# Hybrid gMLP and SSD layer: squares of the last groups three ticks later, a new order of PSUM banks, the fifth unit's normalization behind two evictions, and a new turn of places for the late loads

## The chip, the cores and the metric

The kernel runs on one core of a Trainium2 chip. The metric is the device time of one execution in microseconds. A core has TensorE (PE; its weight loads are shown as PEld), VectorE (DVE), ScalarE (ACT), GpSimd (POOL), and SyncE (SP), whose queue issues most DMAs here. Each engine works through its own instructions in order; across engines they wait for each other by semaphores.

## The reference

One layer, one sequence of 1024 rows, width 1024, all in float32.

```python
h = rms_norm(x, norm_w) * (1 + scale) + shift          # scale, shift, gate from silu(c) @ ada_w + ada_b
gm_u, gm_v, gm_z, ssm_z, xbc, dt_raw, g_a, g_b = split(h @ w_in)
y_a = spatial_gating(gelu(gm_u), gelu(gm_v)) * silu(gm_z)      # chunks of 128, 8 groups
xs, bm, cm = split(silu(causal_depthwise_conv(xbc)))
y_b = ssd_scan(xs, softplus(dt_raw + dt_bias), -exp(a_log), bm, cm) + xs * d_skip
yz  = (y_b * silu(ssm_z)) as 8 groups of 256 columns
y_b = rms_norm(yz, ssm_norm_w) per group
merged = sigmoid(g_a) * (y_a @ w_proj_a) + sigmoid(g_b) * (y_b @ w_proj_b)
out = rms_norm(x + gate * (merged @ w_out), final_norm_w)
```

What matters here: each group's `yz` is squared, summed over its 256 columns, and its rows are scaled by the inverse root of that sum before the product with `w_proj_b`.

## The kernel before, in words

Products are made in float32 accuracy from high and low halves: three matmuls stand for one (`hi*hi`, `hi*lo`, `lo*hi`). Larger products use seven block products (`p1` to `p7`) in place of eight. The stages in time:

- to about 920 us: conditioning, the input projections (L591, L703), convolution and gates;
- about 920 to 1149 us: the SSD scan, 32 steps of a group and a double chunk (8 groups, two by two, 4 steps each), with the products of `w_proj_a` as a fill between them (`pma`, recorded at L91);
- 1149 to 1306 us: projection b, 56 units of 12 matmuls (L1710). A unit is one block product and one k; its four accumulators `x` or `yp` are PSUM banks;
- to the end: the output projection (`ou`, `ow`, L1968), the residual x, the last norm.

From the end of the input projections to the last unit of projection b, `hand[0]` is set: every instruction keeps the place on its engine at which the code wrote it (the wrapper at L56 records them all, so most rows of the profile have that line; matmuls go through the helper at L91, transposes through L94, SyncE's DMAs through L100). After L1906 a scheduler orders the rest.

In the SSD stage the order is set by ticks. A step `n` has three ticks: `front` (the products `yi` inside a chunk and `sp` for the state), `back` (`yn` from the state, `ym`, `y`, and `yz = y * z` on GpSimd) and `prep_products` (`pc`, `px`, from which ScalarE's copy `bn` comes). The exponentials `dcy` of the next steps go to ScalarE in the same ticks. `later(delay, f)` (L506) puts a function so many ticks ahead, and `run_tasks` (L509) runs what is due. `draw` (L1546) puts in fill.

When a group has two steps done, `post` (L1240) puts in, by ticks:

- `leave`: two stores of `yz` to DRAM (`yb_d`, SyncE);
- `squares`: ScalarE squares `yz`, GpSimd adds the two halves. For the first half row of every group (`q == 0`) the squares overwrite `yz` in its place, so they wait for the two stores;
- `post2`: matmuls `pq` with ones; `post2b`: VectorE evicts `pq` into one of three small rows, `cwt`, `tri`, `par` in turn, and SyncE stores that (`ss_d`), loads it back as `ssq`, GpSimd takes the root, SyncE stores it (`rs_d`). From there `rb` is loaded, by which `y_norm` (L1614) scales a loaded block `yn` for a unit of projection b (VectorE `yn<-yn,par,rb`, where `par` is another small tile of that name, of constants).

Banks: `bank` takes the first bank of the list `free`, `release` puts one back at its end. At the start of projection b the eight banks become `q0` to `q7`, and `places_of` (L1828) says which are the four `x` and which the four `yp` accumulators. A bank whose last content is not evicted makes its first matmul wait.

Units: `operands(u)` (L1680) makes the high half `p1bh` and the low half `p1bl` of unit u's block, the same of its weight (`p1a`), and calls `ready(u + 1)` (L1663) between, which normalizes the next unit's block. While the ticks run out, the loop at L1805 makes `operands(0)` to `operands(3)` at `n` = 2, 4, 6, 8.

Places: `gate_slot` (L1595) gives the small tiles of the gates in projection b, and the later loads of x (`xr`, L1920), a place in turn out of eight entries of three pools. A load into a place waits until its last content was read; for x that reader is GpSimd's `add_x` (L1924) or VectorE's add at L1988.

Of the kernel before, what the change touches and what calls it, by code (L numbers as in the profile page):

```python
# [21 lines left out]
NG = 8  # L22
# [13 lines left out]
def hybrid_kernel(  # L36
# [24 lines left out]
    x, out = x[0], out[0]  # L61
# [34 lines left out]
    def f32(t):  # L96
        return t.bitcast(F32)

    def move(dst, src):
        pin(nc.sync.dma_start(dst, src))  # L100
# [42 lines left out]

    hpool = tc.tile_pool(name="hpool", bufs=1, reuse_waits="tile")
    hp = hpool.__enter__()
    BANKS = (1, 2, 4, 0, 3, 6, 5, 7)
    BN = ("b11", "t1", "t2", "b22", "t3", "b21", "t4")
    bop = {}
    for nm in BN:
# [349 lines left out]
    def numbered(pool, c):  # L499
        for b in range(8):  # L500
            pool.tile([P, 512], F32, name=f"{c}{b}_0", tag=f"{c}{b}")
# [4 lines left out]
    def later(delay, f, *a):  # L506
        tasks.append((slot[0] + delay, f, a))

    def run_tasks():  # L509
        slot[0] += 1  # L510
        due = [t for t in tasks if t[0] <= slot[0]]
        for t in due:
            tasks.remove(t)
            t[1](*t[2])
# [565 lines left out]
    class Group:  # L1080
# [159 lines left out]
        def post(self, q):  # L1240

            g = self.g
            yz = self.yz[q]

            def leave():
                for j in range(2):
                    move(yb_d[2 * g + j][:, q * 512 : (q + 1) * 512], yz[:, j])

            if g < NG - 2 or q == 0:
                soon = 0 if g < NG - 2 else 4  # L1250
                later(4, leave)
                later(9 - soon, self.squares, yz, [yz[:, j] for j in range(2)])
                later(17 - 2 * soon, self.post2, q, yz[:, 0])
            else:
                wait = 1 if g < NG - 1 else 3
                later(wait + 3, leave)
                sq = [turn(r, f"sq{g}", F32) for r in ((y1_r, ym_r) if g < NG - 1 else (last_sq, last_sq))]
                later(wait, self.squares, yz, sq, pin)
                later(9, self.post2, q, sq[0])
# [79 lines left out]
    def turn(r, name, dt=F32R):  # L1339
        tags, at = r  # L1340
        at[0] += 1
        return take(name, tags[(at[0] - 1) % len(tags)], dt)
# [81 lines left out]
    p2r = None  # L1424
    for n, (name, _, _, d1, d2, g) in enumerate(todo):
# [12 lines left out]
        if n == len(jobs):  # L1438
# [6 lines left out]
            p2r = p2rpool.__enter__()  # L1445
# [9 lines left out]
        if n + 2 == len(todo):  # L1455
            wspool.__exit__(None, None, None)
            p2xpool = tc.tile_pool(name="p2x", bufs=1, side="right", reuse_waits="tile")
            p2x = p2xpool.__enter__()
# [72 lines left out]
    numbered(psum, "k")  # L1531
    free.extend(BANKS)
    for k in (6, 7):
# [12 lines left out]
    def draw(n):  # L1546
        for _ in range(n):
            left[0] -= next(fill, 1) is None
# [41 lines left out]
    def give(name):  # L1590
        room.append(tags_of.pop(name))

    n_gate = [0]

    def gate_slot(name):  # L1595
        n_gate[0] += 1
        pool, tag, b = ((p2r, "ea", 2), (p2x, "xe", 3), (p2x, "xd", 3), (p2x, "xe", 3), (p2x, "xd", 3), (p2r, "ea", 2),
                        (p2x, "xe", 3), (p2x, "xd", 3))[n_gate[0] % 8]
        return pool.tile([P, 512], F32, name=name, tag=tag, bufs=b)


# [12 lines left out]
    def y_norm(n, h):  # L1614
        t = yt[n, h]
        V.scalar_tensor_tensor(t, t, snw[:, n : n + 1], rbs[n // 2, h], op0=ALU.mult, op1=ALU.mult)

    units = [(nm, k) for nm in ("p1", "p2", "p5", "p3", "p6", "p7", "p4") for k in range(KT)]
# [4 lines left out]
    def loads(u):  # L1623

        nm, k = units[u]
        if nm in fresh:
            n, h = fresh[nm]
            y_load(n + k, h)
        aops[u] = t = big(f"{nm}a{k}", F32R).rearrange("p (v c) -> p v c", v=2)
        if nm in WB:  # L1630
            load(f32(t), wb_d[k][:, WB[nm]])
        else:
            raws[u] = raw = gate_slot(f"{nm}r{k}")
            n = k if nm == "p1" else KT + k
            load(raw, w_proj_b[n * P : (n + 1) * P, 0:512])
# [27 lines left out]
    def ready(u):  # L1663

        nm, k = units[u]
        if nm in fresh:
            n, h = fresh[nm]
            y_norm(n + k, h)
        b11, b12 = yt[k, 0], yt.get((k, 1))
        b21, b22 = yt.get((KT + k, 0)), yt.get((KT + k, 1))  # L1670
        source[u] = {"p1": b11, "p2": b21, "p5": b12, "p3": b22, "p6": b12, "p7": b11, "p4": b21}[nm]
        if nm == "p5":
            V.tensor_sub(b12, b12, b11)
        elif nm == "p6":
            V.tensor_sub(b12, b22, b12)
            give(f"yn{KT + k}_1")
        elif nm == "p7":
            V.tensor_sub(b11, b12, b11)

    def operands(u):  # L1680

        nm, k = units[u]
        t = source.pop(u)
        hi, lo = turn(bh_r, f"{nm}bh{k}"), turn(bl_r, f"{nm}bl{k}")
        A.copy(hi, t)
        if nm not in WB:
            a, raw = aops[u], raws.pop(u)
            A.copy(a[:, 0], raw)
        if u + 1 < len(units):
            ready(u + 1)  # L1690
        V.tensor_sub(lo, t, f32(hi))
        if nm not in WB:
            V.tensor_sub(a[:, 1], raw, f32(a[:, 0]))
        bops[u] = hi, lo
        if nm == "p6":
            V.tensor_sub(yt[KT + k, 0], yt[KT + k, 0], t)
        elif nm == "p7":
            give(f"yn{k}_0")
            give(f"yn{k}_1")
        elif nm == "p4":  # L1700
            give(f"yn{KT + k}_0")
# [13 lines left out]
    def gate_load(b, h):  # L1715
        hs = slice(h * 512, (h + 1) * 512)
        th = gate_slot(f"tg{b}_{h}")
        ma = kept[b, h][0] if (b, h) in kept else gate_slot(f"ma{b}_{h}")
        load(th, th_d[(KT + b) * P : (KT + b + 1) * P, hs])
        if (b, h) not in kept:  # L1720
            load(ma, mt_d[b][:, hs])
        gates[b, h] = th, ma
# [68 lines left out]
    def ahead(u):  # L1791
        if u + LOAD < len(units):
            loads(u + LOAD)
        if u + LEAD < len(units):
            operands(u + LEAD)
# [3 lines left out]
    def ya_free():  # L1799

        while emptied[0] < KT and left[0] <= 3 * (KT - 1 - emptied[0]):
            room.extend(ya_tags[emptied[0]])
            emptied[0] += 1
# [4 lines left out]
    n = 0  # L1808
    while tasks:
        n += 1  # L1810
        draw(2)
        ya_free()
        if n == 1:
            ready(0)
        elif n in (2, 4, 6, 8):
            operands(n // 2 - 1)
        if n in (4, 5, 6, 7):
            loads(n - 1)
        run_tasks()
    draw(left[0] + 1)  # L1820
    ya_free()
    for tags in (war_r[0][0][2:], wah_r[0][0][2:], wal_r[0][0][2:], y1_r[0], ym_r[0]):
        room.extend(tags)
    ps2.__exit__(None, None, None)
    ps3 = tc.tile_pool(name="ps3", bufs=1, space=PSUM, reuse_waits="tile")
    psb = ps3.__enter__()
    numbered(psb, "q")
    places_of = {"x": (0, 1, 3, 2), "y": range(4, 8)}  # L1828
    assert all(b > 3 for b in free[6:])
    OB = {"p1": 0, "p5": 1, "p7": 2, "p4": 3, "p6": 4, "p2": 5, "p3": 6}  # L1830
    OORDER = ("p1", "p5", "p6", "p7", "p4", "p3", "p2")
# [272 lines left out]
```

## Time and profile before

| | us |
|---|---|
| median of three runs | 1393.1 (1392.56 to 1395.51) |
| the profiled execution | 1396.83 |
| its span | 1395.1 |
| mean granted clock of TensorE | 0.995 |
| TensorE busy, share of the span | 98% |
| VectorE, ScalarE, GpSimd busy | 76%, 57%, 16% |
| DMA over the span | 204 GB/s |

The page's first part gives each engine's busy time. The waits of TensorE name the engine and the tile for which it stood still. A timeline row has start, duration, engine, line, operation, tiles (out<-in), form and count, and in brackets the idle time before it with what ended it; a row with a count stands for several in a run. A table of stretches has the granted clock of TensorE for each.

### The profile page before, as it was taken

What the parts mean: (1) busy time and instruction counts of PE and PEld (TensorE: products, weight loads), DVE (VectorE), ACT (ScalarE), POOL (GpSimd) and SP (SyncE); (2) the same over time, 40 slices, a digit from 0 to 9 for tenths busy, and PEclk for the clock granted to TensorE, in tenths of its full rate; (3) what the DMA queues carried; (4) which work ended last, traced back from release to release, by engine and by line L of the source; (5) the groups of instructions that cost most, each with busy time, mean ns of one, the idle gap of its engine ahead of it and who ended that gap; (6) DMA issues with size and microseconds to landing.
All of it is one profiled execution on the core that took longest, in us unless ns stands there. A gap on an engine that the chain in (4) does not pass through costs nothing.

```text
span 1395.1 us, 20387 instructions
## 1 busy us (share of the span) xinstructions
PE 1365.6 (98%) x6955; PEld 1125.6 (81%) x6955; DVE 1058.0 (76%) x1784; ACT 794.2 (57%) x1474; POOL 221.1 (16%) x209
## 2 busy tenths in 40 slices
PE   8999999999999999999999999999999899999987
PEld 7678888888888888888878887888888777888876
DVE  5666766887777678867888988578887777788965
ACT  6664456666656666655556555577877634233543
POOL 0000000000000000000000000018888870000152
PEclk9999999999999999999999999999999999999999
DMA  8565533544322356766657897598898849977452
GB/s 278 153 218 165 174 99 102 176 126 156 121 89 93 121 158 181 205 198 198 190 163 241 277 303 238 177 330 305 292 305 295 277 130 301 397 264 280 145 174 121
DMA packets 272940, 286.58 MB, mean 205 GB/s; under 512 B 18844, under 2 KB 215876, under 8 KB 272836
## 3 DMA queue, kind: packets, MB, share of 16 engines
q1 hardware_dynamic: 196676, 214.35, 48.7%
q10 hardware_dynamic: 76160, 70.92, 14.9%
q8 instruction: 55, 0.90, 0.3%
q14 instruction: 49, 0.40, 0.1%
HBM read 198.77 MB, written 86.44 MB: 204 GB/s over the span
## 4 chain that ended last, share of the span: by engine, by line
PE 82%; DVE 5%; DMA 4%; issue 3%; ACT 3%; POOL 2%; SPq 1%; ACTq 0%; DVEq 0%; POOLq 0%
PE xuz L591 6%; PE xcb L591 6%; PE x L1710 6%; PE xx L591 6%; PE xz L591 5%; PE xg L591 5%; PE yp L1710 5%; PE pma L91 4%; PE yuz L591 3%; PE ycb L591 3%; PE vx L703 3%; PE yx L591 3%; PE yz L591 3%; PE yg L591 2%; PE vy L703 2%
## 5 line engine op out<-in xcount | busy, mean ns | idle before, releaser
L56 POOL TENSOR_SCALAR_AFFINE_SELECT dcy<-dcy 128x1024 f32<-128x1024 f32 x32 | 35.4, 1107 | 782.2 <-DMA yl<-ya_d 734.6
L56 ACT ACTIVATE dcy<-dcy,nacs 128x128 f32<-128x128 f32 x256 | 78.4, 389 | 16.8 <-POOL dcy L56 16.4
L1924 POOL TENSOR_TENSOR r<-r,xr 128x512 f32<-128x512 f32 x12 | 26.6, 2236 | 160.0 <-DMA xr<-in_x_dram 152.1
L56 ACT ACTIVATE ea<-dcy 64x512 f32<-64x512 f32 x64 | 40.3, 630 | 8.1 <-DMA dcy<-acs_d 7.5
L91 PE MATMUL pma<-yh,wah 128*128 128x512 f32 x128 | 42.9, 417 | 0.0
L1029 ACT ACTIVATE ac<-ac 128x1024 f32<-128x1024 f32 x32 | 33.9, 1061 | 15.6 <-DVE ac L1027 15.5
L91 PE MATMUL pma<-yh,wal 128*128 128x512 f32 x128 | 42.6, 414 | 0.0
L56 POOL TENSOR_TENSOR yz<-y,sl 128x512 f32<-128x512 f32 x32 | 41.9, 1309 | 0.6
L56 DVE TENSOR_TENSOR dcy<-dcy,pc 128x1024 f32<-128x1024 f32 x32 | 38.9, 1216 | 2.1 <-PE pc L94 1.2
L56 DVE TENSOR_TENSOR ym<-yn,ea 128x512 f32<-128x512 f32 (+1 forms) x32 | 20.0, 624 | 26.8 <-PE yn L91 26.7
L91 PE MATMUL pma<-yl,wah 128*128 128x512 f32 x128 | 39.9, 393 | 0.0
L56 POOL TENSOR_TENSOR y<-y,ym 128x512 f32<-128x512 f32 (+1 forms) x32 | 38.4, 1199 | 9.5 <-DVE ym L56 9.4
L91 PE MATMUL yi<-dcy,xd 128*64 128x128 f32 x512 | 35.6, 282 | 0.3 <-DVE xd L56 0.3
L1027 DVE SCALAR_TENSOR_TENSOR ac<-c2cb,cwt,ac 128x1023 f32<-128x1023 f32 (+2 forms) x24 | 30.8, 1282 | 6.2 <-ACT ac L1025 6.1
L1027 DVE SCALAR_TENSOR_TENSOR ac<-c2x,cwt,ac 128x1023 f32<-128x1023 f32 (+2 forms) x24 | 30.7, 1280 | 5.2 <-ACT ac L1025 5.1
L91 PEld LDWEIGHTS yi<-dcy,xd 128*64 128x64 f32 x512 | 27.9, 139 | 6.6 <-issue 4.6
L91 PE MATMUL sp<-xe,bn 128*128 128x256 f32 x112 | 32.7, 409 | 0.0
L56 DVE SCALAR_TENSOR_TENSOR yn<-yn,par,rb 128x512 f32<-128x512 f32 x32 | 26.0, 815 | 7.8 <-DMA yn<-yb_d 7.8
L1027 DVE SCALAR_TENSOR_TENSOR ac<-c1x,cwt,ac 128x1023 f32<-128x1023 f32 (+2 forms) x24 | 30.8, 1282 | 0.7 <-ACT ac L1025 0.7
L1027 DVE SCALAR_TENSOR_TENSOR ac<-c1cb,cwt,ac 128x1023 f32<-128x1023 f32 (+2 forms) x24 | 30.8, 1282 | 0.0
L955 ACT CAST wba<-wbr 128x128 fp32r<-128x128 f32 x32 | 9.5, 296 | 36.9 <-DMA wbr<-in_w_proj_b_dram 28.8
L1844 DVE TENSOR_TENSOR wolp<-wolp,wohp 128x512 fp32r<-128x512 f32 x24 | 21.2, 904 | 11.2 <-ACT wohp L1843 11.1
(2913 smaller groups left out, 4391.8 us busy)
## 6 DMA issues: line engine op xcount, KB each, us to landing
sl<-s_d SPq DMA_DIRECT2D x32, 768.0 KB
s_d<-ac ACTq DMA_DIRECT2D x32, 512.0 KB
dcy<-acs_d SPq DMA_DIRECT2D x32, 512.0 KB
aw<-in_ada_w_dram SPq DMA_DIRECT2D x16, 512.0 KB
vp<-in_w_in_dram SPq DMA_DIRECT2D x32, 256.0 KB
wbr<-in_w_proj_b_dram SPq DMA_DIRECT2D x64, 128.0 KB
wb_d<-wbb ACTq DMA_DIRECT2D x32, 256.0 KB
wb_d<-wbc ACTq DMA_DIRECT2D x32, 256.0 KB
```

The lines of the kernel that those rows point to most:

```text
L56: return lambda *a, **k: tc.keep_in_program_order(f(*a, **k))
L91: pin(PE.matmul(acc, l, r, start=first, stop=last))
L591: pin(PE.matmul(ps, lw[:, k * P : (k + 1) * P], r[k], start=first and n + k == 0, stop=n == 2 and k == 3, skip_group_check=not first))
L703: pin(PE.matmul(ps[j], l[k][:, js], r, start=first and k + m == 0, stop=k == 3 and m == 2, skip_group_check=not first))
L955: A.copy(hl[:, :, 0], t)
L1027: V.scalar_tensor_tensor(ac[:, s:], cc[:, : S - s], conv_wt[:, 3 - s, i : i + 1], ac[:, s:], op0=ALU.mult, op1=ALU.add)
L1029: A.activation(ac, ac, AF.Silu)
L1710: pin(PE.matmul(ps[j], a[:, v, js], r, start=first and n + k == 0, stop=n == 2 and k == KT - 1, skip_group_check=not first))
L1844: V.tensor_sub(lo, f32(lo), f32(hi))
L1924: G.tensor_add(rows[t][:, half], rows[t][:, half], xr.pop((t, half.start)))
```

## The change

Four places change.

1. `post`: for the last two groups (6 and 7) and `q == 0`, the squares come 8 ticks behind, not 5, and `post2` 12, not 9.
2. `BANKS` is (1, 2, 0, 4, 3, 6, 5, 7) and the x accumulators lie in (1, 3, 0, 2), where they lay in (0, 1, 3, 2).
3. `operands(3)` no longer calls `ready(4)`; it is called once behind the loop, after the last fill.
4. `gate_slot` uses another order of places.

```diff
-    BANKS = (1, 2, 4, 0, 3, 6, 5, 7)
+    BANKS = (1, 2, 0, 4, 3, 6, 5, 7)
...
             if g < NG - 2 or q == 0:
-                soon = 0 if g < NG - 2 else 4
+                late = g >= NG - 2
                 later(4, leave)
-                later(9 - soon, self.squares, yz, [yz[:, j] for j in range(2)])
-                later(17 - 2 * soon, self.post2, q, yz[:, 0])
+                later(8 if late else 9, self.squares, yz, [yz[:, j] for j in range(2)])
+                later(12 if late else 17, self.post2, q, yz[:, 0])
...
         n_gate[0] += 1
-        pool, tag, b = ((p2r, "ea", 2), (p2x, "xe", 3), (p2x, "xd", 3), (p2x, "xe", 3), (p2x, "xd", 3), (p2r, "ea", 2),
-                        (p2x, "xe", 3), (p2x, "xd", 3))[n_gate[0] % 8]
+        pool, tag, b = ((p2x, "xd", 3), (p2x, "xe", 3), (p2r, "ea", 2), (p2x, "xd", 3), (p2x, "xe", 3), (p2x, "xd", 3),
+                        (p2x, "xe", 3), (p2r, "ea", 2))[{2: 3, 3: 2}.get(n_gate[0], n_gate[0]) % 8]
...
-    def operands(u):
+    def operands(u, then=True):
...
-        if u + 1 < len(units):
+        if then and u + 1 < len(units):
             ready(u + 1)
...
         elif n in (2, 4, 6, 8):
-            operands(n // 2 - 1)
+            operands(n // 2 - 1, n < 8)
...
     draw(left[0] + 1)
     ya_free()
+    ready(4)
...
-    places_of = {"x": (0, 1, 3, 2), "y": range(4, 8)}
+    places_of = {"x": (1, 3, 0, 2), "y": range(4, 8)}
```

On ScalarE, at the end of the SSD scan, the order of the last two groups' third and fourth steps. `yz_0_10611` are the squares of group 6, `yz_0_10701` those of group 7; `dcy` are exponentials, eight in a row, `bn` the copies that TensorE waits for.

```order
 L56 ACTIVATE ea_3_10737<-dcy_3_10733 64x512 x2
+L56 ACTIVATE dcy_3_10733<-dcy_3_10733,nacs 128x128 x8
+L56 COPY bn_2_10894<-pc_2_10867 128x256
+L56 ACTIVATE ea_3_10812<-dcy_3_10808 64x512 x2
+L56 CAST wah_0_10923<-wa_0_10363 128x512
+L56 CAST wah_1_10926<-wa_1_10365 128x512
 L56 ACTIVATE yz_0_10611<-yz_0_10611 128x512 x2
-L56 ACTIVATE dcy_3_10733<-dcy_3_10733,nacs 128x128 x8
-L56 COPY bn_2_10897<-pc_2_10867 128x256
-L56 ACTIVATE ea_3_10812<-dcy_3_10808 64x512 x2
-L56 CAST wah_0_10926<-wa_0_10363 128x512
-L56 CAST wah_1_10929<-wa_1_10365 128x512
```

Group 6's squares stood ahead of the eight exponentials and the copy `bn`; now they stand behind these, an `ea` and two casts of the fill's weights.

On VectorE, where projection b begins, in the kernel before. `cwt` and `tri` are the evictions of the last two `pq`, `yn_0_11217` is the fifth unit's block, `p1bl` and `p1a` are the low halves of the fourth unit's operands.

```order
L56 TENSOR_SCALAR cwt<-pq_1_11242 128x128
L56 SCALAR_TENSOR_TENSOR yn_0_11217<-yn_0_11217,par_152,rb_0_11215 128x512
L56 TENSOR_TENSOR p1bl_11265<-yn_0_11205,p1bh_11264 128x512
L56 TENSOR_TENSOR p1a_11207<-p1r_11208,p1a_11207 128x512
L56 TENSOR_SCALAR tri<-pq_1_11271 128x128
```

The same place in the changed kernel, where the fifth unit's block is `yn_0_11216`:

```order
L56 TENSOR_SCALAR cwt<-pq_1_11240 128x128
L56 TENSOR_TENSOR p1bl_11263<-yn_0_11204,p1bh_11262 128x512
L56 TENSOR_TENSOR p1a_11206<-p1r_11207,p1a_11206 128x512
L56 TENSOR_SCALAR tri<-pq_1_11268 128x128
L56 SCALAR_TENSOR_TENSOR tha_0_11120<-tha_0_11120,pma_0_11164 128x512
L56 SCALAR_TENSOR_TENSOR tha_1_11122<-tha_1_11122,pma_1_11165 128x512
L56 SCALAR_TENSOR_TENSOR yn_0_11216<-yn_0_11216,par_152,rb_0_11214 128x512
```

The normalization of the fifth unit's block moved from ahead of the `tri` eviction to behind it and two `tha`.

On SyncE, the loads of the third to the fifth unit's blocks (`yn<-yb_d`), in the kernel before; `ss_d<-par` is the store of a row of sums, `rs_d<-ssq` that of a row of roots:

```order
L100 DMA ss_d_0_80<-par 4x128
L100 DMA rb_0_11155<-rs_d_59 128x512
L100 DMA yn_0_11157<-yb_d_101 128x512
L100 DMA p1r_11160<-in_w_proj_b_dram 128x512
L100 DMA ssq<-ss_d_0_78 128x4
L100 DMA yb_d_111<-yz_2_10945 128x512
L100 DMA yb_d_112<-yz_2_10945 128x512
L100 DMA rs_d_62<-ssq 128x4
L100 DMA yn_0_11205<-yb_d_102 128x512
```

In the changed kernel:

```order
L100 DMA rb_0_11153<-rs_d_59 128x512
L100 DMA yn_0_11155<-yb_d_101 128x512
L100 DMA p1r_11158<-in_w_proj_b_dram 128x512
L100 DMA yb_d_111<-yz_2_10942 128x512
L100 DMA yb_d_112<-yz_2_10942 128x512
L100 DMA rs_d_62<-ssq 128x4
L100 DMA ss_d_0_80<-par 4x128
L100 DMA yn_0_11204<-yb_d_102 128x512
```

The store of `par` moved from ahead of the third unit's block to just ahead of the fourth unit's, and a load of `ssq` moved behind the latter.

## The prediction

> **What bounds the kernel now.** I read the page first, for who is busy, then the waits of TensorE, then the stretches around each of those waits, and last the rows of the engines that end them.
>
> ```profile
> PE 1365.6 (98%) x6955; PEld 1125.6 (81%) x6955; DVE 1058.0 (76%) x1784; ACT 794.2 (57%) x1474; POOL 221.1 (16%) x209
> PEclk9999999999999999999999999999999999999999
> ```
>
> TensorE is busy for 98% of the span, and the change leaves every engine the number of instructions that it had. So it can gain only where TensorE stands still or runs below its full clock. The view of TensorE's waits over the whole span names the places; the columns are the total, the count and the longest.
>
> ```profile
> PE ou L1968 <- DVE r L1985: 2.8, 1, 2.8
> PE px L94 <- ACT bn L56: 2.8, 1, 2.8
> PE x L1710 <- DVE tri L56: 2.5, 1, 2.5
> ...
> PE ou L1968 <- ACT r L1982: 1.1, 1, 1.1
> ...
> PE yn L91 <- DVE st_home L56: 0.8, 1, 0.8
> PE x L1710 <- DVE cwt L56: 0.4, 1, 0.4
> ```
>
> The program is the same up to the last two groups' front parts (about 1100 us), so only these six, 10.4 us together, lie in its reach. The two `ou` waits belong to the output projection and the `yn` wait to the last state update. The stretches show what a wait costs beside its own length: the columns are the length, busy time of TensorE, its weight loads, VectorE, ScalarE and GpSimd, then the granted clock, DMA share and GB/s.
>
> ```profile
> 1112.00:1116.00 4.00, 1.21 (x9) 0.97 (x8) 0.69 (x1) 3.99 (x13) 1.27 (x1) 0.93 0.40 68
> 1116.00:1120.00 4.00, 4.00 (x34) 3.04 (x32) 1.71 (x3) 3.97 (x10) 3.42 (x4) 0.64 0.01 2
> 1120.00:1124.00 4.00, 4.00 (x29) 3.04 (x28) 2.35 (x6) 1.32 (x5) 4.00 (x5) 1.00 0.04 2
> ...
> 1149.00:1155.00 6.00, 3.38 (x14) 2.51 (x15) 3.29 (x7) 0.03 (x1) 0.05 (x1) 1.00 1.00 315
> ...
> 1349.00:1353.00 4.00, 1.20 (x7) 0.66 (x5) 4.00 (x4) 0.93 (x3) 2.96 (x3) 1.00 0.56 181
> 1353.00:1357.00 4.00, 4.00 (x12) 3.19 (x13) 4.00 (x4) 1.96 (x5) 2.38 (x2) 0.68 0.23 69
> ```
>
> Behind the gap at 1112 the clock falls to 0.64 for about four microseconds, behind the one at 1349 to 0.68; behind the shorter one at 1151 it stays at 1.00.
>
> **Part 1, squares of the last groups further behind their stores.** The timeline of ScalarE, one row of GpSimd and one of SyncE (start, duration, what, and in brackets the idle time before with its releaser) tell why `bn` was late.
>
> ```profile
> 1111.53 1.22 ACT L56 ACTIVATE yz<-yz 128x512 f32<-128x512 f32 x2 [7.80 <-DMA yb_d<-yz]
> 1112.66 2.43 ACT L56 ACTIVATE dcy<-dcy,nacs 128x128 f32<-128x128 f32 x8
> 1114.99 0.35 ACT L56 COPY bn<-pc 128x256 f32<-128x256 f32 x1
> ```
> ```profile
> 1104.66 1.08 POOL L56 TENSOR_SCALAR_AFFINE_SELECT dcy<-dcy 128x1024 f32<-128x1024 f32 x1
> ```
> ```profile
> 1106.31 0.90 SPq L100 DMA_DIRECT2D yb_d<-yz  x2
> ```
>
> The squares overwrite `yz` in its place, so they wait for the stores of `yz`, issued at 1106.31, which end 5.2 us later. Eight exponentials and the copy `bn` queue behind them, and TensorE behind `bn`. In the new order the exponentials, `bn`, `ea` and two `wah` casts stand ahead of the squares. The input of the exponentials is ready at 1104.66 + 1.08 = 1105.74; eight take 2.43, and `bn` ends near 1108.5. TensorE wants it at 1112.6. The wait of 2.79 goes, and nothing is next: four microseconds are left.
>
> What the gap costs behind itself is read from TensorE's rows, which hold the same sequence (px, pc, pc, px, pq, yi, sp) twice.
>
> ```profile
> 1106.18 0.38 PE L94 MATMUL px<-ident,sl 128*128 128x128 f32 x2
> ...
> 1109.20 0.81 PE L91 MATMUL pma<-yh,wal 128*128 128x512 f32 x2
> ...
> 1115.39 0.65 PE L94 MATMUL px<-ident,sl 128*128 128x128 f32 x2 [2.79 <-ACT bn L56]
> ...
> 1120.31 0.43 PE L91 MATMUL pq<-yz,ones 128*32 128x128 f32 x8
> ```
>
> The first time it takes 1109.20 - 1106.18 = 3.02 us, behind the gap 1120.31 - 1115.39 = 4.92. The difference, 1.90, is the low clock, and it goes with the gap. **Part 1 gives 2.79 + 1.90 = 4.69.**
>
> On the clock the Trainium skill ("TensorE: Matmul & The Clock Gate", "Why this matters for your kernels") advises no idle gaps of TensorE above some 3 us. Both gaps of 2.8 us in this trace lie below that and the clock fell behind each, so the trace puts the point lower, between 2.5 and 2.8; by the page's figure the 1.90 would not belong to the gap, which is a rival below.
>
> What the moved instructions do now: the squares still may wait for their stores, but at the end of a row of other work (bn 1108.5, ea and two casts to about 1111), so for some 0.5 us. Behind them on ScalarE stand the other group's exponentials and the next `bn`, ending near 1115.5 (the same 3.8 us from squares to `bn` as in the rows above); the matmuls that need that `bn` come behind the `pq` of 1120.31, which is 1115.6 once 4.69 is gone, so it is in time. GpSimd's sums of squares and the matmuls `pq` slide along by three ticks; they feed `tri` and `par`, small VectorE evictions, whose rows go out on SyncE for units that come much later. The `yn <- st_home` wait of 0.8 stays: its chain (y, yz, state, yn) is not touched, and I cost it at nothing.
>
> **Parts 2 and 3, the start of projection b: the banks, and the fifth unit's normalization.** Rows of VectorE, of TensorE and of SyncE.
>
> ```profile
> 1146.83 0.75 DVE L56 SCALAR_TENSOR_TENSOR yn<-yn,par,rb 128x512 f32<-128x512 f32 x1 [2.08 <-DMA yn<-yb_d]
> ...
> 1148.71 0.28 DVE L56 TENSOR_SCALAR cwt<-pq 128x128 f32<-128x128 f32 x1
> 1151.71 0.75 DVE L56 SCALAR_TENSOR_TENSOR yn<-yn,par,rb 128x512 f32<-128x512 f32 x1 [2.72 <-DMA yn<-yb_d]
> ...
> 1153.58 0.29 DVE L56 TENSOR_SCALAR tri<-pq 128x128 f32<-128x128 f32 x1
> ```
> ```profile
> 1149.13 0.47 PE L1710 MATMUL x<-p1bh,p1a 128*128 128x512 f32 x1 [0.36 <-DVE cwt L56]
> ...
> 1151.05 0.39 PE L1710 MATMUL x<-p1bh,p1a 128*128 128x512 f32 x1
> 1153.92 0.50 PE L1710 MATMUL x<-p1bh,p1a 128*128 128x512 f32 x1 [2.49 <-DVE tri L56]
> ```
> ```profile
> 1141.97 0.38 SPq L100 DMA_DIRECT2D yn<-yb_d  x1
> ```
>
> The first x block lies in the bank that `cwt <- pq` empties, the fourth in that of `tri <- pq`. With the new table the first lies in another bank, and the bank of `cwt` is a y bank, wanted twelve matmuls later at the earliest: **0.36 goes**. The fourth x block still waits for `tri`. Ahead of `tri` stood the fifth unit's normalization, which waited 2.72 for its load. It now stands behind. Starting from the fourth unit's normalization at 1146.83, `cwt` comes 1.88 later, then 0.2, two operands at 0.6 each, and `tri` at 1150.1, done by 1150.45. The fourth block is due at 1151.05 + 0.24 = 1151.29 less the 0.36, 1150.93. So in the old frame 2.63 goes whole (1153.92 - 1151.29), with half a microsecond to spare. But TensorE arrives 4.7 us earlier, and the load has to follow. SyncE now issues the store of `par` (0.5 us) just ahead of it, and that eats the spare time. Bounds: nothing left to wait, or 2.63 when the load doesn't move up at all. I take 0.25, near the lower end, because the row ahead of that load, a store of `ssq`, comes out of the same GpSimd chain that is no longer held. **0.36 + 2.63 - 0.25 = 2.74.**
>
> The normalization that moved is wanted four units on, at 2.7 us a unit, and waits for a load anyway; units six to nine have 1 to 3 us by the same reckoning. Cost nothing; if that cover is gone, what is late of them is paid once.
>
> **Part 4, the places.** In the tail some loads of x wait for other adds of GpSimd. Two rows of VectorE, two of GpSimd:
>
> ```profile
> 1345.28 7.04 DVE L1844 TENSOR_TENSOR wolp<-wolp,wohp 128x512 fp32r<-128x512 f32 x6 [2.19 <-ACT wohp L1843]
> 1352.24 0.68 DVE L1985 TENSOR_TENSOR r<-r,ou 128x512 f32<-128x512 f32 x1
> ```
> ```profile
> 1346.85 4.92 POOL L1924 TENSOR_TENSOR r<-r,xr 128x512 f32<-128x512 f32 x3 [1.36 <-ACT r L1982]
> 1352.81 1.29 POOL L1924 TENSOR_TENSOR r<-r,xr 128x512 f32<-128x512 f32 x1 [1.04 <-DMA xr<-in_x_dram]
> ```
>
> The load ahead of the add at 1352.81 now waits for an add that ends earlier, so this one may begin at 1346.85 + 4.92 = 1351.77, beside VectorE's last subtractions ahead of `r` (1352.24), on which TensorE waits 2.8. Those six ran at 7.04 / 6 = 1.17 each beside GpSimd against about 0.68 for the row next to them. The loss lies between nothing and one add, 1.29; nothing excludes a small gain from loads that come earlier. I take -0.4: only the last subtraction or two meet it. The two `ou` waits stay.
>
> **The sum**: 4.69 + 2.74 - 0.4 = **7.0 us**. The profiled execution took 1396.83 with a span of 1395.1, so it would become 1389.8 with a span near 1388.1. It lies 3.7 above the median of 1393.1; the waits are of DMAs and handoffs that I have no reason to think longer in it, so I take the same off the median: **1386.1**.
>
> **The rivals.**
>
> *The second wait stays.* `tri` still stands behind a load, the fourth unit's. If that load leaves no earlier than before (its SyncE row held by a store that waits for `ssq`), the fourth x block waits as long as it did, and parts 2 and 3 give nothing: 4.69 - 0.4 = 4.3, **1388.8**. For it speaks the 2.08 that VectorE waited for this load already; against it, that the queue was held by what part 1 frees. 0.12.
>
> *The low clock is not the gap's.* If 1116 to 1120 runs at 0.64 for another reason, the gain is 7.0 - 1.9 = 5.1, **1388.0**. This is where the page's 3 us would lead. Against it are two gaps of 2.8 with a fall behind each and none elsewhere near. 0.06.
>
> *SyncE is held at the moved store of `par`*, which would make it slower. Rows of SyncE, GpSimd and VectorE:
>
> ```profile
> 1111.28 0.50 SPq L100 DMA_DIRECT2D ss_d<-par  x1
> 1119.25 0.32 SPq L100 DMA_DIRECT2D rs_d<-ssq  x1
> ```
> ```profile
> 1118.21 1.01 POOL L56 TENSOR_TENSOR ssq<-ssq,nhalf 128x4 f32<-128x4 f32 x1
> ```
> ```profile
> 1138.07 2.58 DVE L56 SCALAR_TENSOR_TENSOR yn<-yn,par,rb 128x512 f32<-128x512 f32 x2
> ```
>
> SyncE works in order, and the trace has such a hold: from 1111.78 to 1119.25, 7.5 us, behind one store that waited for GpSimd's `ssq`. The store of `par` now stands ahead of the fourth unit's load and all later loads, and `par` is evicted between the first two normalizations: these start at 1138.07 - 4.7 = 1133.4, so `par` comes near 1135. SyncE gets there at about 1141.97 - 4.7 - 0.5 = 1136.8, two microseconds later. Each microsecond beyond that is paid at the fourth x block. The gains without the rest of that wait are 7.3; to lose them and 2.8 more the load must be some 10.4 late, `par` after 1147. At 11 the time is 1393.1 - 7.3 + 10.6 = **1396.4**. Before, `tri` and `par` were evicted well ahead of need, which speaks against it. 0.05.
>
> *The waits come back in another place*: the gaps close, but the next things in the chain (state, `yn`, later units' loads) are late by as much, and the time stays at **1393**, with a fall of the clock again behind one gap. Engines other than TensorE have idle time throughout (VectorE 76%), which speaks against it. 0.09.
>
> **How the numbers follow.** The forecast has 0.68. A measurement of this kernel can tell some 0.2%, 2.8 us, from no change. Faster by more than that are the forecast and the first two rivals: 0.68 + 0.12 + 0.06 = 0.86; the last gives 0.09 for the same, the third 0.05 for slower. The lower end is 1393.1 - 7.7 (nothing left at the fourth block, no loss in the tail) less 1 for the medians' own spread: 1384.4. The upper end is the first rival with the tail's full 1.29, 1389.7, and 0.8 for that spread: 1390.5. It leaves out the last two rivals, 0.14.
>
> **What would show it.** Part 1: no `px <- bn` wait, ScalarE's wait for `yb_d` below 1 us in place of 7.80, and a clock of 1.00 all through 1104 to 1124; a low clock there without a gap gives the second rival. Parts 2 and 3: the first x matmul near 1144, no `x <- cwt`, `x <- tri` at 0.6 or less; 2 or more gives the first rival, and 8 or more with SyncE idle ahead of `ss_d <- par` the third. Part 4: `ou` waits of 2.8 and 1.1, up by 1.3 at most. The forecast is wrong as a whole if a wait of over 2 us stands at a place that is not in the list above.

## The result, and the profile after

The changed kernel takes 1387.68 us (median of 22 runs, 1385.79 to 1394.44); the kernel before, over its own 22 runs, 1391.76 us (1388.26 to 1396.70). The ratio is 0.9974 with a 95% interval of 0.9964 to 0.9984: 3.6 us faster, 2.2 to 5.0 by the interval (the two medians lie 4.1 apart). The forecast was 7.0 us faster and 1386.1 us, in a range of 1384.4 to 1390.5. The direction and the range held; the gain is about half of what was worked out.

The profiled execution of the changed kernel took 1394.44 us, its span 1392.7; it is the slowest of the 22. First its waits of TensorE from 860 us on (total, count, longest):

```profile
PE ou L1969 <- DVE r L1986: 3.0, 1, 3.0
PE ou L1969 <- ACT r L1983: 1.0, 1, 1.0
PE yn L91 <- DVE st_home L56: 0.8, 1, 0.8
PE yn L91 <- POOL yz L56: 0.5, 1, 0.5
```

The three waits that the change was costed by, `px <- bn`, `x <- tri` and `x <- cwt`, are not there; the one at `yn` for `yz` ends at 1031.12, far ahead of what was moved. The stretches (length, busy time of TensorE, its weight loads, VectorE, ScalarE, GpSimd, then granted clock, DMA share, GB/s):

```profile
1112.00:1116.00 4.00, 4.00 (x40) 3.19 (x39) 4.00 (x9) 3.11 (x9) 3.64 (x5) 1.00 0.96 361
1116.00:1120.00 4.00, 4.00 (x45) 3.48 (x45) 2.50 (x5) 3.88 (x11) 3.44 (x5) 1.00 0.51 140
1120.00:1124.00 4.00, 4.00 (x25) 3.32 (x22) 2.62 (x7) 1.42 (x3) 3.54 (x4) 1.00 0.04 3
...
1149.00:1155.00 6.00, 6.00 (x29) 4.95 (x28) 3.72 (x7) 1.14 (x2) 0.00 (x0) 1.00 0.96 311
...
1349.00:1353.00 4.00, 2.38 (x8) 1.87 (x9) 4.00 (x5) 2.03 (x6) 3.80 (x3) 0.82 0.19 62
1353.00:1357.00 4.00, 4.00 (x15) 3.24 (x14) 2.32 (x5) 2.10 (x7) 0.00 (x0) 0.75 0.01 2
```

TensorE is busy without a break through the first four, at a clock of 1.00; the gap and the low clock in the tail are as before. ScalarE's rows (start, duration, what, idle time before and its releaser) show why:

```profile
1110.49 2.45 ACT L56 ACTIVATE dcy<-dcy,nacs 128x128 f32<-128x128 f32 x8 [1.54 <-POOL dcy L56]
1113.79 0.37 ACT L56 COPY bn<-pc 128x256 f32<-128x256 f32 x1 [0.85 <-DVE dcy L56]
1114.06 1.27 ACT L56 ACTIVATE ea<-dcy 64x512 f32<-64x512 f32 x2
1115.35 1.14 ACT L56 CAST wah<-wa 128x512 fp32r<-128x512 f32 x2
1116.40 1.14 ACT L56 ACTIVATE yz<-yz 128x512 f32<-128x512 f32 x2
```

The exponentials and `bn` run as soon as their input is there. The squares of `yz` come 5.9 us later and find their stores landed; the 7.80 us for `yb_d` have no successor.

VectorE at the start of projection b, and two rows of SyncE:

```profile
1139.30 0.28 DVE L56 TENSOR_SCALAR par<-pq 128x128 f32<-128x128 f32 x1
...
1146.00 0.75 DVE L56 SCALAR_TENSOR_TENSOR yn<-yn,par,rb 128x512 f32<-128x512 f32 x1 [0.81 <-DMA yn<-yb_d]
...
1149.28 0.28 DVE L56 TENSOR_SCALAR tri<-pq 128x128 f32<-128x128 f32 x1
```
```profile
1142.40 0.49 SPq L100 DMA_DIRECT2D ss_d<-par  x1
1142.99 0.39 SPq L100 DMA_DIRECT2D yn<-yb_d  x1
```

`tri` is done at 1149.56, and TensorE's tenth matmul of projection b, which needs its bank, is due at 1149.55 + 9 x 0.23 = 1151.6. `par` is there 2.8 us before SyncE gets to its store, and the load behind it goes out at once.

**Where the two profiles differ.** Four starts on TensorE split each span: a matmul of the last input projection, the `pq` of the fifth group, the first x matmul, the first ou matmul. The rows of before, but for the x matmul, whose row stands in the prediction (1149.13):

```profile
883.62 1.07 PE L591 MATMUL xg<-b11h,p1g12h 128*128 128x512 f32 x4
...
1107.04 0.43 PE L91 MATMUL pq<-yz,ones 128*32 128x128 f32 x8
...
1305.10 0.39 PE L1968 MATMUL ou<-wohp,ma11h 128*128 128x512 f32 x1
```

And those of the changed kernel:

```profile
890.09 1.07 PE L591 MATMUL xg<-b11h,p1g12h 128*128 128x512 f32 x4
...
1112.59 0.43 PE L91 MATMUL pq<-yz,ones 128*32 128x128 f32 x8
...
1149.55 0.39 PE L1710 MATMUL x<-p1bh,p1a 128*128 128x512 f32 x1
...
1302.53 0.39 PE L1969 MATMUL ou<-wohp,ma11h 128*128 128x512 f32 x1
```

Up to the first row the program is the same, and this execution was 6.5 us later there; that is luck. From `pq` to x it is 42.09 before and 36.96 after, 5.13 less; from x to ou 155.97 and 152.98, 2.99 less; from ou to the end 90.0 and 90.17. So in this pair of profiles the change is worth 7.95 us, more than forecast. The ratio of all runs says 3.6. The question for the runs is which of the two a plain execution has, and why.

### The profile page after: what moved, and what is told of

The parts are those of the page before. It is cut to its first block, busy times and chain, and to the rows that moved or that the text cites. A ratio compares the mean times of both kernels' runs of the same rounds, so it can differ in the third digit from the quotient of the medians.

```text
span 1392.7 us, 20386 instructions
## 1 busy us (share of the span) xinstructions
PE 1362.8 (98%) x6955; PEld 1122.0 (81%) x6955; DVE 1054.2 (76%) x1784; ACT 794.3 (57%) x1474; POOL 223.0 (16%) x209
## 3 DMA queue, kind: packets, MB, share of 16 engines
q1 hardware_dynamic: 196676, 214.35, 48.8%
## 4 chain that ended last, share of the span: by engine, by line
PE 63%; DMA 13%; DVE 10%; issue 5%; ACT 4%; POOL 2%; SPq 2%; ACTq 0%; DVEq 0%; POOLq 0%
PE x L1710 6%; PE xuz L591 6%; PE yp L1710 5%; PE xcb L591 4%; PE pma L91 4%; PE xx L591 4%; PE yuz L591 3%; PE vx L703 3%; DMA wbr<-in_w_proj_b_dram 3%; PE xg L591 3%; PE vy L703 2%; PE ycb L591 2%; PE xz L591 2%; SPq L100 2%; PE yx L591 2%
```

## The experiments

All ratios are against the kernel before, run beside them on the same chip. The unchanged kernel, run as if it were another, came out at 1.002 with an interval that leaves out 1 (below), so each ratio near 1 is to be read with some 0.2%, 2.8 us, of doubt beyond its interval; the stretches of the profiles are sharper.

**The kernel before again**, unchanged, three more times. Theory A: the waits of the first profile are a fixed part of the kernel. Rival B: they were long in that one execution.

> The kernel before, unchanged, for a second profile of it. Theory A (the waits are a fixed part of the kernel): from the first xg matmul of unit 12 (883.62 in the first profile) to the end of the span the second profile has again about 511.5 us, with the px <- bn wait near 2.8, the clock at 0.6 to 0.7 behind it and x <- tri near 2.5. Rival B (the first profile of before was an unlucky execution, its DMA waits larger than usual): the same stretch takes 507 to 509 us, the px <- bn wait is below 2 or the clock stays at 1.00 behind it. Ratio to before 1.000.

> The kernel before, unchanged, one more look. The px <- bn wait was 2.8, 2.0 and 0.8 in three programs that are the same up to there. If the landing of the stores sets it (theory B), it is again another number between 0 and 3, equal to ScalarE's wait for yb_d less about 5; if it is fixed at 2 to 2.8 (theory A) the 0.8 was due to the other edits. The stretch from the first xg matmul of unit 12 to the end: 506 to 511.5 us.

> As the third look: the px <- bn wait anywhere between 0 and 3 by theory B, 2 to 2.8 by theory A. On the clock: a gap of 2 us or more is followed by a granted clock below 0.85 in some looks and by 1.00 in others, if the fall depends on where the gap lies in a free-running window; by 0.6 to 0.7 each time from 2.8 on, if it depends on the length alone.

The second measured 1393.99 us (median of 12; ratio 1.002, 1.0008 to 1.0031), the third 1388.96 and the fourth 1391.07 (one run each). TensorE's waits from 1100 us on, in the second and then in the third:

```profile
PE x L1710 <- DVE tri L56: 2.4, 1, 2.4
...
PE px L94 <- ACT bn L56: 2.0, 1, 2.0
```
```profile
PE ou L1968 <- DVE r L1985: 2.8, 1, 2.8
PE x L1710 <- DVE tri L56: 1.5, 1, 1.5
PE px L94 <- ACT bn L56: 1.4, 1, 1.4
```

And the stretch with the px wait and the one behind it, in the second and then in the third:

```profile
1112.00:1116.00 4.00, 2.33 (x23) 1.74 (x25) 0.07 (x1) 3.96 (x11) 1.51 (x3) 0.81 0.05 16
1116.00:1120.00 4.00, 4.00 (x29) 2.85 (x26) 3.44 (x8) 3.60 (x11) 4.00 (x5) 0.76 0.03 3
```
```profile
1108.00:1112.00 4.00, 2.61 (x35) 2.00 (x35) 0.69 (x1) 3.96 (x11) 1.51 (x2) 1.00 0.20 48
1112.00:1116.00 4.00, 4.00 (x30) 2.78 (x27) 3.10 (x6) 3.94 (x12) 4.00 (x6) 1.00 0.03 3
```

By the terms set for it the second profile spoke for theory A: 510.57 us from the xg matmul to the end of the span (511.48 in the first), a px wait of 2.0, and a fall of the clock behind it. The third and the fourth decide: 506.57 and 508.09 us, a px wait of 1.4 in both, and a clock (the last column but two) of 1.00 behind it. Theory A is out: both the wait and what it does to the clock differ from execution to execution, and the first profile had the longest of all. As expected of the landing of the stores, the px wait goes with ScalarE's wait for `yb_d`: 7.80, 6.85, 6.64 and 6.35 us there, 2.79, 2.00, 1.39 and 1.43 here, some 5 us less each time. On the clock the fourth answers what was asked of it: behind a gap of 2.26 us it stays at 1.00, behind one of 2.70 it falls, both in the tail of one execution.

**The changed kernel again**, unchanged.

> The changed kernel, unchanged, for a second profile. Theory A: the same stretch takes 502.6 us again, as in the first profile of it (890.09 to 1392.7), while what lies ahead of it, where the program is the same, differs from profile to profile by some us. Rival B': the changed kernel's own late waits vary, 502 to 507. Ratio 0.9974 as measured before, 0.994 by the difference of the two first profiles in that stretch (8.9 us).

Measured: 1386.80 us (8 runs), ratio 0.9967 (0.9953 to 0.9981). From `pq` to x 36.99 us, from x to ou 153.01, to the end 90.05, all within 0.2 of its first profile, and 502.32 from the xg matmul to the end (502.61 in the first). So the changed kernel's late stages repeat; those of before don't.

**One part without the other.**

```diff
 # squares, banks and x places changed; not these:
-    ready(4)                          # behind the loop
-    gate_slot's new turn
```

> Squares three ticks later and the new banks and x places; the fifth unit's normalization and the places of the late loads as before. Theory A: no px <- bn wait, clock 1.00 from 1104 to 1124, x <- cwt gone, x <- tri stays at 2.5 to 2.8: a gain of 5.0 us, ratio 0.9964. Rival B: the gap was a lucky find of one profile, gain 1 to 2.5, ratio 0.998 to 0.999. Rival on the order: with TensorE earlier by 4.7 the load ahead of tri moves up less, x <- tri 4 or more, gain below 4.

Measured: 1388.57 us (12 runs), ratio 0.9978 (0.9965 to 0.9992). No px wait, 36.97 from `pq` to x, as in the whole change; then, among its waits:

```profile
PE ou L1968 <- DVE r L1985: 3.1, 1, 3.1
PE x L1710 <- DVE tri L56: 1.5, 1, 1.5
```

The `tri` wait is 1.5, not the 2.5 of the first profile nor the 4 of the rival: with the normalization ahead of the eviction it is there, but smaller, as large as in the third and fourth profile of before. The gain is 3.1 us by the ratio, 5.0 was expected.

```diff
 # banks, x places and ready(4) changed; not these:
-    squares at 8 and 12 ticks
-    gate_slot's new turn
```

> New banks and x places and the fifth unit's normalization behind the tri eviction; squares and places of the late loads as before. Theory A: px <- bn stays at 2.8 with a clock of 0.6 to 0.7 behind it; x <- cwt and x <- tri below 0.3: a gain of 2.9 us, ratio 0.9979. Rival: the wait comes back at the fourth unit's load, x <- tri 1 or more, gain below 2, ratio 0.9987 or more.

Measured: 1389.32 us (12 runs), ratio 0.9986 (0.9973 to 0.9999). No wait at the start of projection b, 153.08 from x to ou. The px wait stays, at

```profile
PE px L94 <- ACT bn L56: 0.8, 1, 0.8
```

in this execution. The gain is 1.9 us by the ratio, 2.9 was expected; within the 0.2% of doubt that is no proof of a gain, and the stretch from x to ou has to stand for it. So, by one profile of each, each part takes away its own wait: the squares the one at px, the normalization with the banks the one at x. With the squares goes one more, of 0.6 us at `yn` for `st`, some 20 us behind `pq`, which is there in this run and in four of the six profiles of before.

**The stores earlier, in place of the squares later.**

```diff
-                later(4, leave)
+                later(4 - soon // 2, leave)     # two ticks earlier for groups 6 and 7
```

> The kernel before, but the stores of yz of groups 6 and 7 (first half row) two ticks earlier; the squares stay where they are. If the squares' wait for these stores is the whole cause of the px wait, ScalarE's wait for yb_d shrinks by 2 to 5 us and px <- bn goes as it did with the squares moved: ratio 0.9975 to 0.9985, clock 1.00 from 1104 to 1124. If ScalarE's order of work is what matters and the stores only stand by, px <- bn stays above 0.8. Rival: SyncE waits for yz on GpSimd with the next step's loads behind it, and dcy or sl come late: a new wait of TensorE of 1 us or more, ratio 1.000 or above.

Measured: 1394.12 us (11 runs), ratio 1.0013 (1.0002 to 1.0024): not faster, where 0.9975 to 0.9985 was expected. ScalarE's rows, and TensorE's waits:

```profile
1107.18 1.19 ACT L56 ACTIVATE yz<-yz 128x512 f32<-128x512 f32 x2 [4.39 <-DMA yb_d<-yz]
1108.28 2.44 ACT L56 ACTIVATE dcy<-dcy,nacs 128x128 f32<-128x128 f32 x8
1110.63 0.34 ACT L56 COPY bn<-pc 128x256 f32<-128x256 f32 x1
...
1115.88 0.63 ACT L56 ACTIVATE yz<-yz 128x512 f32<-128x512 f32 x1 [2.53 <-DMA yb_d<-yz]
```
```profile
PE x L1710 <- DVE tri L56: 2.6, 1, 2.6
PE yn L91 <- ACT bn L56: 2.2, 1, 2.2
```

The first group's squares start 1.1 us behind `pq` in place of the 4.5 of the first profile, and the px wait is gone: it is the landing of the stores that sets it. But the same knot stands one group later. The second group's squares now wait for their own stores, with the next exponentials and `bn` behind them, and TensorE waits 2.2 at `yn`, with a clock of 0.64 behind:

```profile
1120.00:1124.00 4.00, 4.00 (x28) 3.67 (x30) 2.83 (x5) 0.00 (x0) 2.06 (x2) 0.64 0.02 5
```

In the first profile of before the second group's squares, held back by the first wait, come 10.5 us behind `pq` (1117.58) and wait for nothing; here they stand ready earlier, and their stores let them go 9.8 us behind it. So that second wait was covered by the first. The change moves the squares of both groups behind the exponentials, and neither wait comes back. The rival named for this run (the next step's loads late behind SyncE's wait) wasn't the one that showed.

**The places alone.**

```diff
 # gate_slot's new turn, nothing else
```

> The kernel before with the new turn of places alone. By the prediction 0.4 us slower, bounds 0 to 1.3, which the times can't tell from nothing: ratio 0.9995 to 1.001. In the profile the fifth of GpSimd's last adds starts 1 us nearer to the first ou matmul than before (46.7 in place of 47.7 us behind it), and VectorE's r for which TensorE waits comes at 47.1 (no cost) or up to 48.4 (the full bound).

Measured: 1391.03 us (12 runs), ratio 0.9991 (0.9974 to 1.0009): no difference that can be told. From ou to the end 89.35. In this profile the waits in the tail had another split than in the first one (ou <- ACT r 2.1, ou <- DVE r 1.2), so the two starts named in the expectation can't be compared one by one: `r` comes 48.2 us behind the first ou matmul, close to the upper bound, but behind a longer wait for ACT's `r` and a fall of the clock. The whole changed kernel shows them:

```profile
1342.94 7.04 DVE L1845 TENSOR_TENSOR wolp<-wolp,wohp 128x512 fp32r<-128x512 f32 x6 [3.44 <-ACT wohp L1844]
1349.89 0.68 DVE L1986 TENSOR_TENSOR r<-r,ou 128x512 f32<-128x512 f32 x1
```
```profile
1344.51 8.29 POOL L1925 TENSOR_TENSOR r<-r,xr 128x512 f32<-128x512 f32 x5 [1.36 <-ACT r L1983]
```

GpSimd's last five adds now run without the breaks that stood ahead of the fourth and the fifth, as predicted; VectorE's six subtractions take 7.04 as before, and `r` comes 1349.89 - 1302.53 = 47.36 behind the first ou matmul, before 1352.24 - 1305.10 = 47.14. These 0.2 us were lost ahead of the subtractions, which begin that much later (40.41 and 40.18 behind the first ou matmul, both times behind ScalarE's `wohp`). All profiles with the x loads on SyncE say the same: where the wait for ACT's `r` is short, the matmul that waits for VectorE's `r` starts 47.9 to 48.3 us behind the first ou matmul with the old places (five profiles) and 48.1 and 48.2 with the new; where that wait is 2.0 or more, 48.8 and 49.0 with the old and 48.9 with the new. The places cost nothing that can be seen.

**The late loads of x on another queue.** Both kernels keep a wait of about 3 and one of about 1 in the tail. Read as a theory: SyncE works in order, and stands at a load of x until GpSimd has freed its place, with the next weights (`wolp`) behind it. SyncE's rows of before:

```profile
1317.99 0.42 SPq L100 DMA_DIRECT2D xr<-in_x_dram  x1
1318.50 0.38 SPq L100 DMA_DIRECT2D wolp<-wo_d  x1
1332.17 0.33 SPq L100 DMA_DIRECT2D xr<-in_x_dram  x1
```

It issues nothing for 13.3 us (1318.88 to 1332.17).

```diff
-        load(r, x[t * P : (t + 1) * P, half])
+        nc.gpsimd.dma_start(r, x[t * P : (t + 1) * P, half])
```

> The changed kernel, with the late loads of x issued from GpSimd's queue in place of SyncE's. The two ou waits (3.0 and 1.0 to 1.2) are read as SyncE held at a load of x whose place GpSimd's slow adds (15.07 us for four) have not freed, with the wolp loads behind it. If so the wolp loads leave 5 us or more earlier, ou <- ACT r goes and ou <- DVE r falls below 1: ratio 0.994 or less against before, some 4 us below the changed kernel. If VectorE's subtractions are late for the contention alone, ou <- DVE r stays above 2. Rival: issuing costs GpSimd time and the adds come later, ratio 0.998 or more.

> The kernel before with the late loads of x on GpSimd's queue. The queue edit took the stretch from the first ou matmul to the end from about 90.0 to 83.9 us in the changed kernel; if it works apart from the change, the same here, with px <- bn (0.8 to 2.8) and x <- tri (1.5 to 2.5) still there: ratio 0.9955, some 6 us below before. If the changed places are needed for it, the tail stays at 86 or more and the ratio at 0.998 or above.

> The changed kernel with the late loads of x on GpSimd's queue, once more, on the same chip as the kernel before with it. With the noise of the tail gone from both, the difference of the two is the change without its tail: 5.5 to 7 us by the mean of the profiles' stretches (four of before, two of the changed kernel, up to the first ou matmul), 3.5 to 4.5 if the medians measured so far are the truth and the profiles overstate it. Ratio 0.992 again.

> As the run before, but without the new turn of places. If the places have no effect of their own, the same time within 0.1%, and 83.9 from the first ou matmul to the end; if the new turn is what lets the loads run ahead once SyncE is free, 1 to 2 us slower.

Measured: the changed kernel with this edit 1381.18 us (6 runs, ratio 0.9924, 0.9910 to 0.9938) and 1380.94 us (6 runs, 0.9917, 0.9893 to 0.9942); the kernel before with it 1386.51 us (8 runs, 0.9951, 0.9929 to 0.9972); without the new places 1383.25 us (6 runs, 0.9924, 0.9897 to 0.9950). SyncE, GpSimd and VectorE of the first of them:

```profile
1304.62 24.40 SPq L100 DMA_DIRECT2D wolp<-wo_d  x14
```
```profile
1310.06 13.13 POOL L1925 TENSOR_TENSOR r<-r,xr 128x512 f32<-128x512 f32 x1 [1.62 <-ACT r L1981]
```
```profile
1328.58 5.91 DVE L1845 TENSOR_TENSOR wolp<-wolp,wohp 128x512 fp32r<-128x512 f32 x6
1334.41 0.68 DVE L1986 TENSOR_TENSOR r<-r,ou 128x512 f32<-128x512 f32 x1
```

GpSimd's add beside VectorE is still slow, but the weights run past it: SyncE issues fourteen `wolp` loads with no load of x between them. `r` comes 1334.41 - 1295.59 = 38.8 us behind the first ou matmul in place of 47.1, both ou waits are gone, and from ou to the end it is 83.91, 83.90, 83.88 and 83.89 in the four profiles against about 90. The theory holds, with or without the new places, which have no effect of their own in the stretch. The median without the new places is 2.3 us (0.17%) above the one with them, where 0.1% was expected; the two ranges overlap (1380.38 to 1384.77 and 1380.51 to 1385.43), and from `pq` to ou the two profiles take 190.06 and 189.99 us, so no stretch looked at holds the difference. The changed kernel with this edit is the fastest here, 0.8% below before.

It also serves the first question: with both ou waits gone from both kernels, the change is worth 1386.51 - 1380.94 = 5.6 us between the medians of eight and six runs beside each other. The means lie 4.5 apart, and by the spread of these runs anything from about 2 to 7 us is possible. The kernel before with this edit still has px <- bn (1.3) and x <- tri (2.2), as expected.

**All profiles together**, in us between the starts on TensorE that were used above. The second column is how far behind `pq` the first group's squares start on ScalarE.

| kernel | squares | px wait | pq to x | x <- tri | x to ou |
|---|---|---|---|---|---|
| before, first | 4.5 | 2.8 | 42.09 | 2.5 | 155.97 |
| before, second | 3.6 | 2.0 | 40.69 | 2.4 | 157.27 |
| before, third | 3.0 | 1.4 | 39.28 | 1.5 | 154.83 |
| before, fourth | 3.0 | 1.4 | 39.29 | 1.5 | 154.82 |
| before, x on GpSimd's queue | 3.0 | 1.3 | 39.26 | 2.2 | 155.63 |
| before, places alone | 3.1 | 1.3 | 39.22 | 1.6 | 154.91 |
| normalization and banks | 2.4 | 0.8 | 38.67 | none | 153.08 |
| stores earlier | 1.1 | none, 2.2 at yn | 41.41 | 2.6 | 157.33 |
| squares and banks | moved | none | 36.97 | 1.5 | 154.84 |
| changed, first | moved | none | 36.96 | none | 152.98 |
| changed, second | moved | none | 36.99 | none | 153.01 |
| changed, x on GpSimd's queue | moved | none | 37.00, 36.96 | none | 152.96, 153.03 |
| the same without the new places | moved | none | 36.96 | none | 153.10 |

In the seven profiles with a px wait it is the start of the squares behind `pq` less 1.6 to 1.8 us. The change takes the first stretch to 37.0 from 39.2 to 42.1 (mean of the first six rows 40.0), and the second to 153.0 from 154.8 to 157.3 (mean 155.6): 3.0 and 2.6 on the mean, 5.6 together, and 4.1 together against the shortest. The times say 3.6 and 4.6 by the ratios of the changed kernel and 4.5 to 5.6 by the last runs. The first pair of profiles said 7.95. From the xg matmul to `pq`, where little but the banks differs, it is 221.7 to 223.4 us in these six and 221.6 to 222.5 in the changed kernel.

## Why the prediction was right, and where it was off

*Part 1, the mechanism*: right. The squares' wait for the stores held the exponentials and `bn`; with the squares behind them the px wait is gone in every profile, and between `pq` and x no other wait came in its place. The moved squares still wait for their stores in some executions, 1.2 us in the run with squares and banks and 0.8 in the one without the new places, and no wait of TensorE follows from it; the prediction had put 0.5 us there at no cost. The run with the stores earlier, and the px wait following the squares' start through seven profiles, show that the landing of the stores is the cause.

*Part 1, the size*: this term failed. I put 2.79 + 1.90 = 4.69 on it, from one execution, and said that its waits are "of DMAs and handoffs that I have no reason to think longer in it". There was a reason: that execution was 3.7 us above the median, and a wait that ends with a DMA's landing can be what differs. Seven profiles with the old order have px waits of 2.79, 2.00, 1.43, 1.39, 1.35, 1.29 and 0.8; in five of them the clock doesn't fall. Where 5.05 was worked out for the stretch from `pq` to x (4.69 and the 0.36 of the `cwt` wait), the first profile loses 5.1 there against the changed kernel, the six of before 3.0 on the mean, and four of them 2.2 to 2.3. Of these 2.3 only 1.4 are the px wait; 0.6 are the wait at `yn` for `st`, which the first profile doesn't have and the prediction couldn't see. The 0.36, too, was there in the first profile and not in the next three. The reading that the clock falls from a length between 2.5 and 2.8 us on was wrong as well: 2.00 was enough, and 3.06 not always (last section).

*Parts 2 and 3*: of the 2.74 worked out, 2.63 - 0.25 = 2.38 lie behind the first x matmul. There the first pair shows 2.99, the mean 2.6, and three of the six 1.8 to 1.9. The `tri` wait went whole; the 0.25 that I left for the fourth unit's load was not needed, since that load took 3.0 us from issue to use (1142.99 to 1146.00) and not 4.9 as before. Here, too, the wait that went was smaller in half of the executions (1.5 to 1.6) than in the first (2.5), and the mean is lifted by the second profile, in which the clock fell behind it.

*Part 4*: -0.4 worked out, nothing that profiles or times can tell. The fourth of GpSimd's last adds did begin earlier; VectorE didn't become slower for it.

*The rivals.* The second wait didn't stay. SyncE was not held at the store of `par`: 1142.40 for the store against 1139.30 + 0.28 for the row, 2.8 us to spare, two had been reckoned. The rival on the clock failed as it was put (the falls come behind gaps, none elsewhere in these stretches), but the sum with the full 1.90 was wrong as well: in most executions it is not paid. That the waits would come back elsewhere was wrong.

*Luck.* The time came within 1.6 us of the forecast, while the gain is 3.4 short of it: the median of three runs from which the sum started was 1.3 us above that of 22. And the range held because its upper end was made for another reason, a `tri` wait that stays, and not for a px wait that is shorter in most executions.

Why the stores land sooner or later stays open, but the record says where to look. From the end of SyncE's two issues to the start of the squares it is 4.3 us in the first profile and 3.2, 3.1 and 2.4 in the next three, while the moment of the issue, against `pq`, differs by less and not in step (0.2, 0.4, -0.1 and 0.6). So most of the difference is in the landing and not in SyncE. The DMA engines were busy for 0.9 or more of that time in all four, so their total load doesn't tell the executions apart, and which transfers stand ahead of the stores wasn't looked at.

## What to carry to other kernels

A wait that ends with a DMA's landing is a distribution, not a number: before a gain is put on it, profile the kernel again, and see where an execution above the median has its excess. In the first profile of before it lay in these waits; the changed kernel's first profile was the slowest of its 22 runs, and its late stretches were as in all others. An operation in place that waits for a store belongs behind the work that others wait for on its engine, and for every group at once, since the next group's wait hides behind the first. A queue that works in order is held by its slowest place: in the tail, moving the loads that wait for a slow engine to that engine's own queue gave more (6 us) than the whole change.

## What the runs showed of the hardware that was not expected

Whether the clock falls behind a gap of TensorE isn't decided by the gap's length. In the profiles' late stages, eighteen gaps lasted 2.0 to 3.1 us; behind fourteen the granted clock fell, behind four it stayed at 1.00, among them the longest, 3.06 us in the run with squares and banks. Behind the sixteen gaps of 1.0 to 1.6 us it never fell.

What decides, by these profiles, is how the gap lies to a grid in time. Each of the fourteen falls is to 0.50, and lasts 3.41 us (once twice that). The three falls in the second profile of before:

```profile
1114.48:1117.89 3.41, 3.41 (x28) 2.46 (x27) 1.32 (x2) 3.39 (x9) 3.03 (x4) 0.50 0.00 0
1152.02:1155.43 3.41, 3.41 (x10) 2.66 (x9) 2.44 (x4) 1.14 (x2) 0.00 (x0) 0.50 0.69 157
1339.76:1343.17 3.41, 3.41 (x10) 2.64 (x9) 2.35 (x2) 1.36 (x3) 2.08 (x2) 0.50 1.04 396
```

Their starts are 37.54 and 225.28 us behind the first, 11.0 and 66.0 times 3.413, and in every profile with more than one fall the starts lie on such a grid. With the grid laid through each profile's falls (where the late stages have none, through the one at the kernel's very end), the 34 gaps part without an exception:

| most of the gap that lies in one window of 3.41 us | gaps | the clock behind it |
|---|---|---|
| 1.98 to 2.80 us | 14 | 0.50 for 3.41 us or twice that |
| 1.59 to 1.84 us (gaps of 2.20 to 3.06) | 4 | 1.00 |
| up to 1.55 us | 16 | 1.00 |

So a fall costs about 3.41 / 2 = 1.7 us by this count, or nothing. Where the grid lies against the program differs between the four profiles of before, and nothing in the runs shows a way to set it: for one execution it is luck, while a single gap of up to 1.84 us didn't bring a fall wherever it lay.

The Trainium skill ("TensorE: Matmul & The Clock Gate", "What's actually happening") calls the window in which activity is counted free-running, and the count of slow matmuls different from run to run; the grid agrees with that. What the Trainium skill says of gaps (on the same page, "Why this matters for your kernels": none above some 3 us) does not: 2.00 us was enough here, and 3.06 not always.

One GpSimd add of 128x512 took 13.13 us while VectorE worked without a break for all but its last microsecond, against 1.29 us for the same add later on; VectorE's subtractions in the tail of before took 1.17 us each beside GpSimd's adds (7.04 for six), in place of 0.69 for one alone.
